# Ordering edges behind the low halves, and other paces for the depthwise convolution and its LayerNorm, in a two-layer decoder step

## The chip, the core and the metric

The kernel runs on one core of a Trainium2 chip. The metric is the device time of one execution in microseconds (us). Engines are named as in the profile: PE is TensorE's matmul stream and PEld its weight load, DVE is VectorE, ACT is ScalarE, POOL is GpSimd, SP is SyncE, which issues most transfers.

## What is computed

One inference step of a two-layer decoder trunk for 256 prompt tokens and 8 x 8 sample tokens, d_model 1024, all in float32. Each layer adds a half-weighted SwiGLU, a mixer with three branches (pooling, convolution, cross-attention into 256 memory tokens) and a second SwiGLU. The change touches the convolution branch. Cut to what matters:

```python
def conv_module(v, buf, w_dw, b_dw, ln_g, ln_b, w_pw):
    a, gate = jnp.split(v, 2, axis=-1)
    z = a * jax.nn.sigmoid(gate)
    ext = jnp.concatenate([buf.astype(z.dtype), z], axis=1)
    y = lax.conv_general_dilated(ext, w_dw[:, None, :], window_strides=(1,), padding='VALID',
        dimension_numbers=('NWC', 'WIO', 'NWC'), feature_group_count=CONV_WIDTH)   # 31 taps a channel
    y = jax.nn.silu(layernorm(y + b_dw, ln_g, ln_b))
    return y @ w_pw, ext[:, -CONV_BUF:]
...
def trunk_layer(x, ...):
    x = x + 0.5 * swiglu_ffn(rmsnorm(x, ffn1_norm), ffn1_w_gu, ffn1_w_down)
    h = rmsnorm(x, mix_norm)
    u, v, q, gl = jnp.split(h @ w_in, ...)
    merged = gates[:, :, 0] * y_pool + gates[:, :, 1] * y_conv + gates[:, :, 2] * y_att
    x = x + merged @ w_out
    x = x + 0.5 * swiglu_ffn(rmsnorm(x, ffn2_norm), ffn2_w_gu, ffn2_w_down)
```

## The kernel before

**Data and matmuls.** Channels lie on the 128 partitions in 8 blocks (`KB`), the T = 320 tokens (256 prompt, 64 sample) along the free axis. Every large matmul is done as three: a weight block is split into a high half `whi` and a low half `wlo`, the operand into `xh` and `xl`, and `chain` (L298) adds hi·xh + hi·xl for the blocks at hand (lines L306, L307) and then lo·xh (L309). A unit is 8 blocks of weights, so 24 matmuls of 128x320.

**Weights.** SyncE brings raw weights in pieces of 1 MB into 4 buffers (`Stream.issue`, L205), along with the sample group's keys (`in_kc`) and values (`in_vc`). A piece holds two units. `split` makes the halves three units ahead of use: the high half is a cast on ScalarE (L232), the low half a subtract on VectorE, raw minus high. VectorE's instructions all go through a helper, so all of them carry its line, L124. While `share` is on (in the parts that use `w_in`), every even unit takes another way: ScalarE casts the high half (L225) and writes its negative into the low half's place (L226), and GpSimd issues a transfer that accumulates onto it (L227).

**The mixer** goes through these parts in the order of the program: memory keys; the GLU part, which makes `z` block by block (`zfin`); memory values (`kv_values`); the queries; four pool groups, each with the columns `u` (copied to `ut`, L773), pool sums `us`, the gate of branch A, the prompt's softmax rows (`mx`, `sm`, `ex`, L602, L607) and the sample group's scores from the keys (L640); the gate of branch C in 8 steps (`sgc`, L831, L832), with the sample group's values (L665) and its output `exo` (L673), which TensorE transposes (L677); the gate of branch B in 8 steps (`sgb`, L861); the projection of the convolution branch, which reads `chi` and `clo`; and `w_out`.

**The convolution** runs beside all this. `conv_gen` (L541) is a generator. Two lanes (`conv_lane`, L494) each take every second of the 8 blocks: 31 taps a block, each one VectorE instruction that multiplies 256 columns of `z` by a constant and adds the running sum `cv` in PSUM; the second lane starts 15 steps late. GpSimd does the sample columns (`conv_sample`). Then come the sum over blocks `ysum`, the LayerNorm in some 13 steps (the mean and the variance by TensorE matmuls with ones, L354; subtraction, squares on ScalarE, reciprocal root on VectorE), and, after the third step of the gate of B, the scaling by `lnr`, Silu on ScalarE (L586) and the split into `chi` (L587) and `clo`.

**What sets the order.** The program is written in an order, and a scheduler then fixes each engine's list when the kernel is built. The written order comes from pacing: before each unit, `pump` gives every side task as many steps as its rate says, `RC` = 3.0 a unit for the convolution and its LayerNorm, `RN` = 6.0 from the Silu part on:

```python
task[2] += task[1]            # task = [generator, rate, credit]
while task[2] >= 1.0:
    task[2] -= 1.0
    if next(task[0], "end") == "end":
```

Of the kernel before, what the change touches and what calls it, by code (L numbers as in the profile page):

```python
# [7 lines left out]
F32 = mybir.dt.float32  # L8
# [3 lines left out]
ALU = mybir.AluOpType  # L12
# [5 lines left out]
TP = 256  # L18
# [14 lines left out]
LA = 3  # L33
NBIG = 8
C_LEAD = 24
RC = 3.0
RN = 6.0
RS = 2.0
RP = 2
# [1 line left out]
C_G1, C_GM, C_G2, C_GK, C_PS, C_BD, C_LG, C_LB, C_WD = 0, 8, 16, 24, 32, 40, 48, 56, 64  # L41
# [43 lines left out]
def trunk_kernel(  # L85
# [42 lines left out]
    dve = Timed(nc.vector, "dve", 1.04, 70.0)  # L128
    pool = Timed(nc.gpsimd, "pool", 2.2, 80.0)

    def nm(s):
        uid[0] += 1
        return f"{s}_{uid[0]}"
# [32 lines left out]
    def ccol(l, off, i):  # L166
        c = l * C_LAYER + off + i
        return cst[:, c:c + 1]
# [4 lines left out]
    class Stream:  # L173
# [45 lines left out]
        def split(self, u):  # L219
            c, half = seq[u // 2], u % 2  # L220
            raw = self.piece("w", c)[:, half * 1024:half * 1024 + 1024]
            hi = wp.tile([P, 1024], F32R, name=nm("whi"), tag="whi")
            lo = wp.tile([P, 1024], F32R, name=nm("wlo"), tag="wlo")
            if self.share and u % 2 == 0:
                nc.scalar.copy(hi[:, :], raw)  # L225
                nc.scalar.mul(lo[:, :], raw, -1.0)  # L226
                nc.gpsimd.dma_start(lo[:, :], w_in[c][:, half * 1024:half * 1024 + 1024], accum_op=ALU.add)  # L227
            else:
                n = 512 if u == 0 else 1024
                for e in range(0, 1024, n):  # L230
                    h, r = hi[:, e:e + n], raw[:, e:e + n]
                    nc.scalar.copy(h, r)  # L232
                    dve.tensor_tensor(out=lo[:, e:e + n], in0=r, in1=h.bitcast(F32), op=ALU.subtract)
            self.units[u] = (hi, lo)
            if half == 1:
                self.done("w", c)
# [37 lines left out]
    side = {}  # L274
# [20 lines left out]
            side.pop(name, None)  # L295

    ws = Stream()

    def chain(out, xs, n):

# [192 lines left out]
    def conv_lane(l, z, y, blocks, zdone, cdone):  # L493

        for j in blocks:
            while j not in zdone:
                yield
            zt = z[j // 4][:, j % 4, :]
            acc = psum("cv", 2)
            dve.tensor_scalar(out=acc[:, :TP], in0=zt[:, 0:TP], scalar1=ccol(l, C_WD, j), scalar2=ccol(l, C_BD, j),  # L500
                              op0=ALU.mult, op1=ALU.add)
            yield
            for k in range(1, TAPS):
                dst = acc[:, :TP] if k < TAPS - 1 else y[j][:, :TP]
                dve.scalar_tensor_tensor(out=dst, in0=zt[:, k:k + TP], scalar=ccol(l, C_WD, k * 8 + j),
                                               in1=acc[:, :TP], op0=ALU.mult, op1=ALU.add)
                yield
            cdone.append(j)

# [31 lines left out]
    def conv_gen(l, z, zdone, ch, gate):  # L541
# [6 lines left out]
        n = 0  # L548
# [11 lines left out]
        dve.tensor_tensor(out=ysum[:, :], in0=y[0], in1=y[1], op=ALU.add)  # L560
        for j in range(2, KB):
            dve.tensor_tensor(out=ysum[:, :], in0=ysum[:, :], in1=y[j], op=ALU.add)
        yield
        sc = tp.tile([P, 1280], F32, name=nm("lns"), tag="pr", bufs=1)
        work = [sc[:, i * T:(i + 1) * T] for i in range(4)]
# [9 lines left out]
        r = tp.tile([P, T], F32, name=nm("lnr"), tag="ysum", bufs=1)  # L575
# [6 lines left out]
        hi, lo = ch[0]  # L582
        for j in range(KB):
# [5 lines left out]
            if j > 0:  # L589
                dve.tensor_tensor(out=lo[:, j - 1, :], in0=y[j - 1], in1=hi[:, j - 1, :].bitcast(F32),  # L590
                                        op=ALU.subtract)
            yield
        dve.tensor_tensor(out=lo[:, KB - 1, :], in0=y[KB - 1], in1=hi[:, KB - 1, :].bitcast(F32),
                                op=ALU.subtract)
# [88 lines left out]
    def mixer(l, mh, acc, on_block):  # L683
# [27 lines left out]
        for j in range(KB):  # L711
# [7 lines left out]
            def zfin(j=j, pa=pa, sg=sg):  # L719
# [4 lines left out]
                if j == 0:  # L724
                    start("conv", conv_gen(l, z, zdone, ch, gate), RC)

# [162 lines left out]
    h, st, on_block = deferred_norm(0, C_G1, squares=False)  # L889
# [15 lines left out]
    for l in range(L):  # L905
# [16 lines left out]
        h, st, _ = mbox[0]  # L922
        mean = lambda st=st: mean_bc(st.acc[:, :], T)
        if l + 1 < L:
# [8 lines left out]
            h, st, _ = nxt[0]  # L933
# [128 lines left out]
```

## Time and profile before

| | |
|---|---|
| median of 3 runs | 1659.61 us (1659.60 to 1660.29) |
| the profiled execution | 1659.87 us, span 1657.9 us |
| granted TensorE clock, mean over the span | 0.997 |
| PE busy | 1630.5 us, 98% |
| DVE busy | 1120.4 us, 68% |
| ACT busy | 784.0 us, 47% |
| POOL busy | 266.7 us, 16% |

The span is the time from the first to the last instruction of the profiled execution; the device time is 2 us longer. A busy time is the sum over an engine's instructions, and a matmul's end is modelled, so TensorE's waits are read from the view of waits and not from its busy time. One layer's mixer takes its taps from 284 to 451 us, the other's from 1097 to 1266 us.

### The profile page before, as it was taken

How to read it: one execution, taken by the hardware profiler on the slowest of the kernel's cores; microseconds unless marked ns; L12 is line 12 of the kernel's file. 1: busy time of each engine (PE TensorE's matmuls, PEld its weight loads, DVE VectorE, ACT ScalarE, POOL GpSimd, SP SyncE). 2: the span in 40 equal slices, each digit the busy share in tenths (PEclk: the TensorE clock that was granted, in tenths of full speed). 3: DMA queues.
4: the chain of work that ended last, by engine and by line, in shares of the span. 5: the costliest groups of instructions: out<-in, count | busy, mean ns of one | idle time of the engine just before them, and what ended most of it. 6: DMA issues, size and time to landing. Idle time of an engine off the chain costs nothing.

```text
span 1657.9 us, 27271 instructions
## 1 busy us (share of the span) xinstructions
PE 1630.5 (98%) x11194; PEld 1585.8 (96%) x11194; DVE 1120.4 (68%) x1854; ACT 784.0 (47%) x1167; POOL 266.7 (16%) x292
## 2 busy tenths in 40 slices
PE   8999999999999999999999999999999999999996
PEld 7999999998889999999999999999988899999996
DVE  7555647999975675554565564579998757655543
ACT  5444534456665444443344443354566544444341
POOL 2000001677520000000000000046674000000000
PEclk9999999999999999999999999999999999999998
DMA  7444446978976444444444444577798754444430
GB/s 276 153 151 145 169 169 199 266 231 238 294 260 229 151 155 151 144 146 149 149 153 153 153 153 166 189 220 232 235 278 254 267 199 153 145 145 147 150 126 32
DMA packets 47325, 305.73 MB, mean 184 GB/s; under 512 B 5728, under 2 KB 5792, under 8 KB 14048
## 3 DMA queue, kind: packets, MB, share of 16 engines
q1 hardware_dynamic: 38160, 270.75, 45.4%
q0 software_dynamic: 8752, 32.90, 9.2%
q8 instruction: 88, 1.44, 0.3%
q10 hardware_dynamic: 288, 0.33, 0.1%
q14 instruction: 37, 0.30, 0.0%
HBM read 295.14 MB, written 8.82 MB: 183 GB/s over the span
## 4 chain that ended last, share of the span: by engine, by line
PE 86%; DVE 7%; issue 3%; DMA 3%; ACT 1%; POOL 0%; DVEq 0%; SPq 0%; ACTq 0%; POOLq 0%
PE mm L306 19%; PE mm L309 19%; PE mm L307 19%; PE cv L309 8%; PE cv L306 8%; PE cv L307 8%; DVE cv L124 3%; DMA raw<-in_kc 2%; DVE us L124 1%; DVE wlo L124 1%; PE sa L665 1%; PE mm L484 1%; PE mm L483 1%; PE mm L487 1%; PE st L837 1%
## 5 line engine op out<-in xcount | busy, mean ns | idle before, releaser
L124 DVE TENSOR_TENSOR wlo<-raw,whi 128x1024 fp32r<-128x1024 f32 (+1 forms) x403 | 498.6, 1238 | 196.2 <-PE mm L309 85.7
L232 ACT CAST whi<-raw 128x1024 fp32r<-128x1024 f32 (+1 forms) x403 | 420.6, 1045 | 428.3 <-PE mm L307 252.9
L306 PE MATMUL mm<-hhi,whi 128*128 128x320 f32 x1712 | 512.3, 313 | 7.6 <-ACT hhi L358 5.8
L307 PE MATMUL mm<-hlo,whi 128*128 128x320 f32 x1712 | 507.8, 310 | 0.0
L306 PEld LDWEIGHTS mm<-hhi,whi 128*128 128x128 f32 x1712 | 321.6, 188 | 16.2 <-ACT hhi L358 6.6
L307 PEld LDWEIGHTS mm<-hlo,whi 128*128 128x128 f32 x1712 | 321.8, 188 | 1.9 <-DVE hlo L124 0.6
L309 PE MATMUL mm<-hhi,wlo 128*128 128x320 f32 x1712 | 289.4, 310 | 1.7 <-DMA wlo<-in_w 1.7
L309 PEld LDWEIGHTS mm<-hhi,wlo 128*128 128x128 f32 x1712 | 260.4, 188 | 2.7 <-DMA wlo<-in_w 2.2
L124 DVE SCALAR_TENSOR_TENSOR cv<-z,cst,cv 128x256 f32<-128x256 f32 x464 | 194.6, 476 | 0.2
L307 PE MATMUL cv<-hlo,whi 128*128 128x320 f32 x592 | 175.0, 310 | 0.0
L306 PE MATMUL cv<-hhi,whi 128*128 128x320 f32 x592 | 173.9, 309 | 0.0
L124 POOL MEMSET z<- 128x120 f32 x4 | 0.8, 196 | 820.5 <-PE mm L307 820.5
L124 POOL TENSOR_TENSOR pr<-pr 128x512 f32<-128x512 f32 (+3 forms) x128 | 122.7, 959 | 7.2
L306 PE MATMUL mm<-hidh,whi 128*128 128x320 f32 x418 | 123.9, 309 | 0.0
L307 PE MATMUL mm<-hidl,whi 128*128 128x320 f32 x418 | 123.7, 309 | 0.0
L362 ACT CAST hidh<-up 128x320 fp32r<-128x320 f32 x88 | 40.0, 459 | 159.8 <-DVE up L124 159.8
L307 PEld LDWEIGHTS cv<-hlo,whi 128*128 128x128 f32 x592 | 111.0, 188 | 0.2
L306 PEld LDWEIGHTS cv<-hhi,whi 128*128 128x128 f32 x592 | 110.8, 188 | 0.0
L309 PE MATMUL cv<-hhi,wlo 128*128 128x320 f32 x592 | 98.8, 309 | 0.0
L309 PEld LDWEIGHTS cv<-hhi,wlo 128*128 128x128 f32 x592 | 89.9, 188 | 0.2
L124 DVE TENSOR_TENSOR up<-mm,rstd 128x320 f32<-128x320 f32 x53 | 26.0, 490 | 87.8 <-PE mm L309 87.8
L306 PE MATMUL cv<-hidh,whi 128*128 128x320 f32 x286 | 84.7, 309 | 0.0
(196 smaller groups left out, 2336.2 us busy)
## 6 DMA issues: line engine op xcount, KB each, us to landing
raw<-in_w SPq DMA_DIRECT2D x221, 1024.0 KB, 4.8
wlo<-in_w POOLq DMA_DIRECT2D x42, 512.0 KB, 7.1
raw<-in_kc SPq DMA_DIRECT2D x16, 1024.0 KB, 7.3
raw<-in_vc SPq DMA_DIRECT2D x16, 1024.0 KB, 6.0
out_co<-z POOLq DMA_DIRECT2D x16, 135.0 KB, 6.4
raw<-in_mem SPq DMA_DIRECT2D x2, 1024.0 KB, 4.8
out_mk<-kt POOLq DMA_DIRECT2D x2, 1024.0 KB, 5.1
out_mv<-va POOLq DMA_DIRECT2D x2, 1024.0 KB, 9.5
```

Of the source, the lines that this page charges most:

```text
L124: return op(*args, **kw)
L232: nc.scalar.copy(h, r)
L306: nc.tensor.matmul(out, hi, xh, start=(i + e == 0), stop=False)
L307: nc.tensor.matmul(out, hi, xl, start=False, stop=False)
L309: nc.tensor.matmul(out, lo, xh, start=False, stop=(i + e == last))
L362: nc.scalar.copy(hi, src)
L483: nc.tensor.matmul(pv[mb][:, :], mh[0][:, k, mb * P:mb * P + P], wh, start=(k == 0), stop=False)
L484: nc.tensor.matmul(pv[mb][:, :], mh[1][:, k, mb * P:mb * P + P], wh, start=False, stop=False)
L487: nc.tensor.matmul(pv[mb][:, :], mh[0][:, k, mb * P:mb * P + P], wl, start=False, stop=(k == KB - 1))
L665: nc.tensor.matmul(po[32 * h:32 * h + 32, :256], pp[:, at:at + 32], raw[:, mb * 1024 + h * 256:mb * 1024 + h * 256 + 256], start=(bb == 0 ...
L837: nc.tensor.matmul(pv[:, :TP], vt[:, mb, o * P:o * P + P], kt[:, 2 * hd + mb, :], start=(mb == 0), stop=(mb == 1))
```

## The change

The rate of the convolution's side task falls from 3.0 to 2.8 steps a unit. After the sum over blocks it is set to a new 4.0, so the LayerNorm's steps go faster, until `RN` = 6.0 applies as before. `split` keeps the last low half made on VectorE in `last_lo`, and a new function `behind` adds to each tap but the first of a block an ordering edge on that instruction. Both are on one engine, so the edge is no wait on the chip: it tells the scheduler that the tap must stand behind that low half in VectorE's list. Line numbers shift in the changed kernel (L124 becomes L125, L306 becomes L313, L673 becomes L682).

```diff
--- before.py
+++ after.py
@@ -33,7 +33,8 @@
 LA = 3
 NBIG = 8
 C_LEAD = 24
-RC = 3.0
+RC = 2.8
+RL = 4.0
 RN = 6.0
 RS = 2.0
 RP = 2
@@ -230,7 +231,7 @@
                 for e in range(0, 1024, n):
                     h, r = hi[:, e:e + n], raw[:, e:e + n]
                     nc.scalar.copy(h, r)
-                    dve.tensor_tensor(out=lo[:, e:e + n], in0=r, in1=h.bitcast(F32), op=ALU.subtract)
+                    self.last_lo = dve.tensor_tensor(out=lo[:, e:e + n], in0=r, in1=h.bitcast(F32), op=ALU.subtract)
             self.units[u] = (hi, lo)
             if half == 1:
                 self.done("w", c)
@@ -295,6 +296,12 @@
             side.pop(name, None)
 
     ws = Stream()
+
+    def behind(ins, earlier):
+
+        tc.add_manual_dep(ins.ins, earlier.ins.name,
+                          mybir.DependencyInfo(mybir.DependencyClass.NoSync, mybir.DependencyReason.DATA),
+                          reason="pace")
 
     def chain(out, xs, n):
 
@@ -502,8 +509,9 @@
             yield
             for k in range(1, TAPS):
                 dst = acc[:, :TP] if k < TAPS - 1 else y[j][:, :TP]
-                dve.scalar_tensor_tensor(out=dst, in0=zt[:, k:k + TP], scalar=ccol(l, C_WD, k * 8 + j),
+                tap = dve.scalar_tensor_tensor(out=dst, in0=zt[:, k:k + TP], scalar=ccol(l, C_WD, k * 8 + j),
                                                in1=acc[:, :TP], op0=ALU.mult, op1=ALU.add)
+                behind(tap, ws.last_lo)
                 yield
             cdone.append(j)
 
@@ -560,6 +568,7 @@
         dve.tensor_tensor(out=ysum[:, :], in0=y[0], in1=y[1], op=ALU.add)
         for j in range(2, KB):
             dve.tensor_tensor(out=ysum[:, :], in0=ysum[:, :], in1=y[j], op=ALU.add)
+        side["conv"][1] = RL
         yield
         sc = tp.tile([P, 1280], F32, name=nm("lns"), tag="pr", bufs=1)
         work = [sc[:, i * T:(i + 1) * T] for i in range(4)]
```

The order changes in these places. First, VectorE in the memory values of the first layer (`wlo` a low half, `cv<-z,cst,cv` a tap). Before:

```order
L124 TENSOR_TENSOR wlo_3381<-raw_3113,whi_3380 128x1024
L124 SCALAR_TENSOR_TENSOR cv_3194<-z_2729,cst,cv_3194 128x256
L124 TENSOR_TENSOR ysum_2807<-z_2729 128x320
L124 SCALAR_TENSOR_TENSOR cv_3387<-z_2729,cst,cv_3387 128x256
L124 TENSOR_TENSOR wlo_3408<-raw_3113,whi_3407 128x1024
L124 SCALAR_TENSOR_TENSOR cv_3194<-z_2729,cst,cv_3194 128x256
L124 TENSOR_TENSOR wlo_3437<-raw_3190,whi_3436 128x1024
L124 SCALAR_TENSOR_TENSOR cv_3387<-z_2729,cst,cv_3387 128x256
L124 SCALAR_TENSOR_TENSOR cv_3194<-z_2729,cst,cv_3194 128x256
L124 TENSOR_TENSOR wlo_3467<-raw_3190,whi_3466 128x1024
```

And with the change:

```order
L125 TENSOR_TENSOR wlo_3373<-raw_3109,whi_3372 128x1024
L125 SCALAR_TENSOR_TENSOR cv_3224<-z_2729,cst,cv_3224 128x256
L125 SCALAR_TENSOR_TENSOR cv_2997<-z_2729,cst,cv_2997 128x256
L125 TENSOR_TENSOR wlo_3395<-raw_3109,whi_3394 128x1024
L125 SCALAR_TENSOR_TENSOR cv_3224<-z_2729,cst,cv_3224 128x256
L125 SCALAR_TENSOR_TENSOR cv_2997<-z_2729,cst,cv_2997 128x256
L125 TENSOR_TENSOR wlo_3424<-raw_3184,whi_3423 128x1024
L125 SCALAR_TENSOR_TENSOR cv_3224<-z_2729,cst,cv_3224 128x256
L125 SCALAR_TENSOR_TENSOR cv_2997<-z_2729,cst,cv_2997 128x256
```

The taps between two low halves are two throughout, and the sum over blocks no longer has its first instruction there; over the GLU part the taps between two low halves fall from 9 to 13 down to 5 to 10, and 18 taps fewer have been issued when the memory values end. The taps end later in the program, in the gate of branch C.

Second, VectorE in the pool groups of the first layer, ahead of the low half that follows the second group's pool sums `us`. Before:

```order
L124 SCALAR_TENSOR_TENSOR merged_3908<-mm_4491,cst,merged_3908 128x320
L124 TENSOR_TENSOR us_4522<-us_4519 128x2x268
L124 TENSOR_TENSOR us_4522<-us_4519 128x2x160
L124 SCALAR_TENSOR_TENSOR cv_4230<-z_2730,cst,cv_4230 128x256
L124 SCALAR_TENSOR_TENSOR cv_3961<-z_2730,cst,cv_3961 128x256
L124 TENSOR_TENSOR us_4570<-us_4522 128x2x264
L124 TENSOR_TENSOR us_4570<-us_4522 128x2x128
L124 SCALAR_TENSOR_TENSOR cv_4230<-z_2730,cst,cv_4230 128x256
L124 TENSOR_TENSOR wlo_4552<-raw_4325,whi_4551 128x1024
```

And with the change:

```order
L125 SCALAR_TENSOR_TENSOR cv_4306<-z_2730,cst,cv_4306 128x256
L125 TENSOR_TENSOR us_4502<-us_4499 128x2x268
L125 TENSOR_TENSOR us_4502<-us_4499 128x2x160
L125 SCALAR_TENSOR_TENSOR cv_4046<-z_2730,cst,cv_4046 128x256
L125 SCALAR_TENSOR_TENSOR cv_4306<-z_2730,cst,cv_4306 128x256
L125 TENSOR_TENSOR us_4548<-us_4502 128x2x264
L125 TENSOR_TENSOR us_4548<-us_4502 128x2x128
L125 SCALAR_TENSOR_TENSOR cv_4046<-z_2730,cst,cv_4046 128x256
L125 TENSOR_TENSOR wlo_4532<-raw_4299,whi_4531 128x1024
```

It reads the same: of the 15 instructions between this low half and the one ahead of it, the change only swaps a `us` and a `merged`.

Third, ScalarE at the Silu block of the first layer (`z<-z,cst`), the gate of branch C (`sgc`, `va`) and the copy of the sample output, `exo`. Before:

```order
L586 ACTIVATE z_2730<-z_2730,cst 128x320 x3
L831 ACT_TABLE_LOAD
L831 ACTIVATE sgc_5204<-mm_5173 128x256
L832 ACTIVATE va_3351<-mm_5173 128x64
L831 ACTIVATE sgc_5263<-mm_5230 128x256
L832 ACTIVATE va_3351<-mm_5230 128x64
L232 CAST whi_5272<-raw_5228 128x1024
L232 CAST whi_5330<-raw_5228 128x1024
L831 ACTIVATE sgc_5300<-mm_5269 128x256
L832 ACTIVATE va_3351<-mm_5269 128x64
L673 COPY exo_5336<-sa_5172 128x256
```

And with the change:

```order
L595 ACT_TABLE_LOAD
L595 ACTIVATE z_2729<-z_2729,cst 128x320 x4
L233 CAST whi_5272<-raw_5222 128x1024
L595 ACTIVATE z_2730<-z_2730,cst 128x320 x2
L233 CAST whi_5330<-raw_5222 128x1024
L595 ACTIVATE z_2730<-z_2730,cst 128x320 x2
L840 ACT_TABLE_LOAD
L840 ACTIVATE sgc_5300<-mm_5269 128x256
L841 ACTIVATE va_3345<-mm_5269 128x64
L682 COPY exo_5336<-sa_5153 128x256
```

The block has moved behind two gates: it now starts after `sgc_5263` and ends right ahead of a table load, `sgc_5300` and the copy of `exo`. On TensorE, the transposes of that copy, before:

```order
L307 MATMUL mm_5327<-hlo_2484,whi_5176 128x320
L309 MATMUL mm_5327<-hhi_2483,wlo_5177 128x320 x8
L677 MATMUL st_5368<-cst,exo_5336 128x128 x2
L306 MATMUL mm_5363<-hhi_2483,whi_5233 128x320
L307 MATMUL mm_5363<-hlo_2484,whi_5233 128x320
```

And with the change:

```order
L314 MATMUL mm_5327<-hlo_2484,whi_5157 128x320
L316 MATMUL mm_5327<-hhi_2483,wlo_5158 128x320 x8
L313 MATMUL mm_5363<-hhi_2483,whi_5227 128x320
L314 MATMUL mm_5363<-hlo_2484,whi_5227 128x320
L686 MATMUL st_5368<-cst,exo_5336 128x128 x2
L313 MATMUL mm_5363<-hhi_2483,whi_5227 128x320
```

They have moved two matmuls back, into the next gate's chain. SyncE's list of transfers is the same in both.

## Rows read from the trace of the kernel before

**Rows 1.** The page's first part: busy us, share of the span, instructions.

```profile
PE 1630.5 (98%) x11194; PEld 1585.8 (96%) x11194; DVE 1120.4 (68%) x1854; ACT 784.0 (47%) x1167; POOL 266.7 (16%) x292
```

**Rows 2.** The page's groups by line: busy us, mean ns, idle before and its releaser.

```profile
L124 DVE TENSOR_TENSOR wlo<-raw,whi 128x1024 fp32r<-128x1024 f32 (+1 forms) x403 | 498.6, 1238 | 196.2 <-PE mm L309 85.7
...
L124 DVE SCALAR_TENSOR_TENSOR cv<-z,cst,cv 128x256 f32<-128x256 f32 x464 | 194.6, 476 | 0.2
```

**Rows 3.** Windows: length; PE, PEld, DVE, ACT, POOL busy (count); PEclk, DMA share, GB/s.

```profile
380.00:432.00 52.00, 50.62 (x371) 45.30 (x370) 50.98 (x110) 36.09 (x61) 36.62 (x43) 1.00 0.85 248
432.00:520.00 88.00, 86.99 (x660) 76.72 (x659) 70.51 (x134) 55.57 (x101) 19.09 (x21) 1.00 0.79 280
```

**Rows 4.** Waits of TensorE, 330 to 520 us: us in total, times, longest us.

```profile
PE mm L306 <- ACT ut L773: 0.7, 1, 0.7
PE mm L309 <- DMA wlo<-in_w: 0.7, 1, 0.7
PE st L652 <- ACT exs L607: 0.5, 1, 0.5
PE sa L640 <- DMA raw<-in_kc: 0.4, 1, 0.4
```

**Rows 5.** Waits of TensorE, 1145 to 1335 us.

```profile
PE sa L640 <- DMA raw<-in_kc: 2.5, 2, 1.7
PE mm L306 <- ACT ut L773: 1.4, 2, 1.0
```

**Rows 6.** Waits of TensorE's weight load, 330 to 520 us.

```profile
PEld mm L306 <- DVE wlo L124: 0.4, 1, 0.4
```

**Rows 7.** Timeline of ScalarE, then VectorE: start, us, engine, line, op, [idle before <- releaser].

```profile
432.63 1.05 ACT L232 CAST whi<-raw 128x1024 fp32r<-128x1024 f32 x1 [0.48 <-PE mm L307]
...
437.00 1.21 DVE L124 TENSOR_TENSOR wlo<-raw,whi 128x1024 fp32r<-128x1024 f32 x1
```

**Rows 8.** Timeline of ScalarE in the pool groups, first layer, then second.

```profile
383.13 1.28 ACT L602 ACT_TABLE_LOAD   x1 [6.00 <-DVE mx L124]
...
392.32 1.05 ACT L226 ACTIVATE wlo<-raw 128x1024 fp32r<-128x1024 f32 x1
...
1240.25 0.51 ACT L607 ACTIVATE exs<-exs,sm 128x256 f32<-128x256 f32 x1 [0.83 <-DVE sm L124]
```

**Rows 9.** The chain of waits, 436 to 460 and 1250 to 1270 us: start, us, what.

```profile
436.12 1.17 PE mm L309 x8
...
439.55 11.62 DMA raw<-in_kc
...
1253.67 14.16 DMA raw<-in_kc
```

**Rows 10.** Timeline of the DMA issues on SyncE, then on GpSimd.

```profile
430.39 8.17 SPq L205 DMA_DIRECT2D raw<-in_w  x2
438.65 1.28 SPq L205 DMA_DIRECT2D raw<-in_kc  x2
...
440.93 0.87 POOL L227 DMA_DIRECT2D wlo<-in_w  x1 [0.39 <-issue]
```

**Rows 11.** Window in which the key pieces land, columns as in rows 3.

```profile
448.00:452.00 4.00, 3.61 (x32) 2.25 (x30) 3.93 (x6) 2.42 (x5) 3.90 (x4) 1.00 1.04 351
```

**Rows 12.** Timeline of ScalarE at the Silu block, then of TensorE at the transposes.

```profile
498.42 1.74 ACT L586 ACTIVATE z<-z,cst 128x320 f32<-128x320 f32 x3
500.18 1.28 ACT L831 ACT_TABLE_LOAD   x1
501.47 0.38 ACT L831 ACTIVATE sgc<-mm 128x256 f32<-128x256 f32 x1
...
508.89 0.37 ACT L673 COPY exo<-sa 128x256 f32<-128x256 f32 x1 [1.91 <-PE sa L665]
...
512.37 0.38 PE L677 MATMUL st<-cst,exo 128*128 128x128 f32 x2
```

**Rows 13.** The tile `chi`: weight loads that read it, ns, first and last start.

```profile
L306 PEld LDWEIGHTS mm<-chi,whi x128: 187/188/188, 537.1 to 1380.1; 128*128 128x128 f32 x128
```

## The prediction

> **What bounds the kernel now.** I read the page first, then the stretch in which the taps run, then the waits inside it. The page [rows 1] shows TensorE busy for 98% of the span and VectorE for 68%, so in the mean VectorE has room. The groups by line [rows 2] show what stands side by side on VectorE: 403 low halves of 1.24 us each, and 464 conv taps, 194.6 us together, so 0.42 us a tap. The windows [rows 3] show where the room is missing: from 380 to 432 us VectorE is busy for 98% of the time (50.98 of 52.00 us). There the taps, the softmax rows, the pool sums and the low halves stand in one full queue. In the stretch behind it there is room again (70.51 of 88.00).
>
> The question is whether TensorE pays for that full queue. Its waits [rows 4, 5] answer it: in the stretch with taps and LayerNorm it waits four times in the first layer, 2.3 us together, and four times in the second, 3.9 us. None is for a low half that VectorE made: three are for `ut`, one for `exs`, one for a low half that comes by an accumulating transfer, three for the sample group's keys `raw<-in_kc`. On the weight load's side one wait of 0.4 us for VectorE's low half is listed [rows 6], and no matmul is listed as held by it. So **the change has 6.2 us to win at the most, 0.37% of the time, and 2.9 us of that (0.4 + 2.5) are for the keys' transfers.** The other 3.3 us are 0.2%, which is also about what a measurement of this kernel can tell from no change.
>
> **The sum, part by part.** No arithmetic goes or comes: the same taps, low halves and matmuls are there in another order, and an edge within one engine is no instruction. Both cost 0. What moves is when things happen.
>
> *The low halves.* Fewer taps stand ahead of each in the GLU part, so they come earlier there. By the end of the value part 18 taps have been put off, 18 x 0.42 = 7.6 us of VectorE. Since no matmul waited for these low halves, earlier ones are worth 0. The nearest to a late one stands at 437.00 us: its high half is ready at 432.63 + 1.05 = 433.68, so the subtract starts 3.3 us late [rows 7]. Between it and the low half ahead the new order has the same 15 instructions (the second pair of lists in the change), so it can gain some tenths at most.
>
> *`ut` and the accumulating transfer.* These waits hang on VectorE at second hand. ScalarE stands still for 6.00 us ahead of 383.13 for `mx`, which is queued on VectorE among the taps; the write that must precede the accumulating transfer follows in ScalarE's queue at 392.32 [rows 8]. In the second layer the scaling of `exs` waits 0.83 us for `sm` at 1240.25, and `ut` stands behind it. With up to 7.6 us less ahead of them, `mx` and `sm` come earlier. But from there on VectorE works through the same list and is as full as before until the taps end, so only the part put off is won. For the transfer's wait (0.7) I take −0.4, between 0 and −0.7. Of the 2.1 us for `ut` (0.7 + 1.4) I take about a third, −0.75, between 0 and −2.1, because ScalarE's own work in its queue holds `ut` too. For `exs` (0.5) I take 0: its transposes move behind the next low halves, while the sum over blocks leaves the stretch; between −0.5 and +0.6.
>
> *The sample keys.* The chain of waits [rows 9] leads from both key waits back to TensorE itself. One transfer takes 11.62 us from 439.55, when TensorE has read the key buffer that it refills, the other 14.16 us from 1253.67. No tap stands in that chain. In the first layer SyncE issues two key pieces at 438.65, behind two weight pieces, and the accumulating transfer goes out at 440.93 [rows 10]. If that one goes earlier or later, the keys' transfer shortens or stretches. I take −0.3. The bounds: −2.9 where both waits end, and +2.0 where the first layer's transfer becomes as long as the second's (14.16 − 11.62 = 2.5, less some tenths that stay hidden).
>
> By a rule of the Trainium skill ("Perfetto Trace Analysis", section "Roofline") one core's 16 DMA engines give about 435 GB/s together; by that an estimate for the 3.67 MB in flight there (two weight pieces, two key pieces, half a piece accumulated) is 8.4 us, and the keys would come in time, −2.9 instead of −0.3. In the trace the window in which they land shows 351 GB/s at a DMA share of 1.04 [rows 11]: there it stays below the figure with the engines full.
>
> *The LayerNorm.* From the first tap to the sum over blocks the generator takes 139 steps (15 until the second lane starts, then 4 x 31). At 3.0 a unit that is 46.4 units, at 2.8 it is 49.7, 3.3 more. A unit is 24 matmuls; 8 take 1.17 us [rows 9], so a unit takes 3.5 us and the delay is 11.6 us. Some 13 steps of the LayerNorm at 4 rather than 3 a unit give back 1.1 units, 3.8 us. Net it is 7.8 us later. In the trace the Silu block ends at 498.42 + 1.74 = 500.16 [rows 12]; it now ends near 508, or at 511 if the higher pace gives little. In the new order it stands right ahead of a table load, a gate and the copy of `exo` (1.28 + 0.38 + 0.37 = 2.0 us), so the copy is done between 510 and 513. TensorE's transposes of `exo` ran at 512.37 and move two matmuls back, to 512.7. That makes a new wait of 0 to 0.3 us a layer; I take 0.3 for both together, between 0 and 0.6. The projection that reads the LayerNorm's result starts at 537.1 [rows 13], more than 20 us behind, so its lateness costs nothing there.
>
> Sum: −0.4 − 0.75 + 0 − 0.3 + 0.3 = −1.15 us. The profiled execution took 1659.87 us, 0.26 us above the median of three (1659.61). From its own time the sum gives 1658.7, and against the median 1658.5 us, which I forecast.
>
> **Rivals.**
> 1. *The keys come in time too.* With all the waits of rows 4 and 5 gone it is −6.2 + 0.3 = −5.9, so 1653.7 us; with the other terms as in my sum and only the keys' waits gone, −1.15 + 0.3 − 2.9 = −3.75, 1655.9 us. For it: moving one transfer can take it out of the burst. Against it: SyncE's list is the same, and TensorE itself releases these loads. Chance 0.14.
> 2. *ScalarE is freed wholly.* All waits but the keys' end and `exo` costs nothing: −3.3, 1656.3 us. For it: each of them has a `mx`, a `sm` or the write for a transfer behind it. Against it: VectorE is as full afterwards. Chance 0.12.
> 3. *The Silu block becomes the wait (slower).* If it ends later than 512.7 − 2.0 = 510.7 us, TensorE's in-order queue stands at the `exo` transposes, with the next gate's matmuls behind them. Were the LayerNorm 4 us later than I worked out, because the edges also hold taps behind low halves that are late themselves, the block would end at 512 to 515: 1.3 to 4.3 us a layer. With my other terms (−1.45) that is +1.1 to +7.1, so 1660.8 to 1666.8 us, 1663.8 in the middle. For it: in the new order the copy stands behind the whole block. Against it: a tap lags only as far as its low half does. Chance 0.22.
> 4. *Nothing that counts.* TensorE waits for nothing that is moved: 1659.6 us. I count this with the forecast, 0.52 together.
>
> **How the numbers follow.** Faster by over 0.2% (below 1656.3) is rival 1 and half of rival 2: 0.20. Slower by over 0.2% (above 1662.9) is two thirds of rival 3: 0.15. All the rest, 0.65, is the same. The forecast's own bounds are 1656.3 (all its gains but the keys': −0.7 − 2.1 − 0.5) and 1662.8 (all its losses at once: +0.6 + 2.0 + 0.6). The range for 8 in 10 goes on from there, to 1655.0, which takes in a half of rival 1, and to 1663.5, which takes in almost a half of rival 3: 0.07 and 0.12 are left out.
>
> **What would show it.** Right: VectorE still about 98% busy from 380 to 432 us; no matmul that waits for a low half; shorter waits for `ut` and for the accumulating transfer; a wait for `exo` of at most some tenths near 513 us; the keys' waits where they were. Wrong: the keys' waits gone, or their transfer near 14 us in both layers; a wait for `exo` of over 1.3 us; or a new wait of TensorE for `sm`, `plh` or `pll`, which would mean that VectorE was relieved in one place and became the bound in the next.

## The result, and the profile after

The changed kernel takes 1674.66 us (median of 4 runs, 1671.60 to 1675.45) against 1659.61 us before: ratio 1.0087, 95% interval 1.0075 to 1.0100, so 0.9% slower. The profiled execution took 1675.45 us, 15.6 us more than the one of before.

The busy times of the page, to be read against [rows 1]:

```profile
PE 1635.5 (98%) x11194; PEld 1590.2 (95%) x11194; DVE 1134.1 (68%) x1854; ACT 784.9 (47%) x1167; POOL 272.9 (16%) x292
```

VectorE runs the same 1854 instructions and needs 1134.1 us for them instead of 1120.4. That is the first thing to see: no work was added, and 13.7 us were. The windows that answer to [rows 3], and three of 4 us in the second of them:

```profile
380.00:432.00 52.00, 50.90 (x374) 45.80 (x374) 52.00 (x107) 33.14 (x55) 34.34 (x36) 1.00 0.82 254
432.00:520.00 88.00, 82.48 (x610) 71.49 (x605) 75.50 (x143) 50.56 (x88) 29.03 (x32) 0.96 0.74 252
476.00:480.00 4.00, 3.44 (x11) 3.09 (x12) 3.89 (x8) 2.28 (x7) 0.00 (x0) 0.50 0.66 272
480.00:484.00 4.00, 4.00 (x42) 2.90 (x40) 3.42 (x7) 1.39 (x2) 0.00 (x0) 0.70 0.01 4
484.00:488.00 4.00, 4.00 (x33) 3.79 (x26) 0.22 (x1) 0.00 (x0) 0.00 (x0) 1.00 0.85 309
```

VectorE has not become freer from 380 to 432 us (52.00 of 52.00), GpSimd is busier from 432 to 520 us (29.03 us against 19.09), and TensorE's granted clock is at 0.50, its lower level of 1.2 GHz, from 476 to 480 us. TensorE's waits, in the stretches of [rows 4, 5], the first layer first:

```profile
PE st L661 <- ACT exs L616: 3.0, 1, 3.0
PE mm L313 <- ACT ut L782: 2.3, 2, 1.2
PE sa L649 <- DMA raw<-in_kc: 1.2, 1, 1.2
PE mm L316 <- DMA wlo<-in_w: 1.1, 1, 1.1
```

```profile
PE st L661 <- ACT exs L616: 4.9, 1, 4.9
PE mm L313 <- ACT ut L782: 2.1, 2, 1.7
PE sa L649 <- DMA raw<-in_kc: 0.6, 1, 0.6
```

The wait for `exs`, 0.5 us before and listed in the first layer alone, is now 3.0 and 4.9 us. Lined up matmul by matmul against the trace of before, between points at which both kernels have done the same matmuls, the changed kernel goes from 4.4 us late (the last matmul ahead of the first `exs` transposes, at 467.0 us before) to 9.2 us late (480.7 us), and from 8.5 (1280.0 us) to 16.3 us (1295.7 us) around the second: it loses 4.8 and 7.8 us there, together 12.6 of 15.6 us.

How the stop comes about is read on four engines. VectorE first (start, us, engine, line, operation; what stands between is left out):

```profile
459.72 2.75 DVE L125 TENSOR_TENSOR us<-us 128x536 f32<-128x536 f32 x2
...
464.26 2.77 DVE L125 TENSOR_TENSOR wlo<-raw,whi 128x1024 fp32r<-128x1024 f32 x1
466.95 1.99 DVE L125 TENSOR_TENSOR us<-us 128x512 f32<-128x512 f32 x2
...
471.04 0.42 DVE L125 TENSOR_REDUCE mx<-sa 128x1 f32<-128x256 f32 x1
...
472.50 0.14 DVE L125 TENSOR_SCALAR mx<-mx 128x1 f32<-128x1 f32 x1
...
474.71 0.15 DVE L125 RECIPROCAL sm<-sm 128x1 f32<-128x1 f32 x1
```

GpSimd beside it:

```profile
459.51 4.15 POOL L125 TENSOR_TENSOR pr<-pr 128x512 f32<-128x512 f32 x4
...
464.12 1.83 POOL L125 TENSOR_TENSOR pr<-z,cst 128x960 f32<-128x960 f32 x1
...
466.52 1.67 POOL L125 TENSOR_TENSOR pr<-pr 128x512 f32<-128x512 f32 x1
```

ScalarE, and the TensorE instructions that wait for it:

```profile
470.74 0.73 ACT L813 CAST plh<-us 128x640 fp32r<-128x640 f32 x1 [5.67 <-DVE us L125]
471.37 1.05 ACT L233 CAST whi<-raw 128x1024 fp32r<-128x1024 f32 x1
472.44 1.28 ACT L611 ACT_TABLE_LOAD   x1
473.73 0.47 ACT L611 ACTIVATE exs<-sa,mx 128x256 f32<-128x256 f32 x1
474.10 0.19 ACT L611 ACTIVATION_READ_ACCUMULATOR exs<-sa,mx 128x1 f32 x1
474.31 1.28 ACT L840 ACT_TABLE_LOAD   x1
475.61 0.38 ACT L840 ACTIVATE sgc<-mm 128x256 f32<-128x256 f32 x1
475.89 0.22 ACT L841 ACTIVATE va<-mm 128x64 f32<-128x64 f32 x1
475.99 0.51 ACT L616 ACTIVATE exs<-exs,sm 128x256 f32<-128x256 f32 x1
```

```profile
476.56 0.69 PE L661 MATMUL st<-cst,exs 128*128 128x128 f32 x2 [3.02 <-ACT exs L616]
...
479.28 0.47 PE L314 MATMUL mm<-pll,whi 128*128 128x320 f32 x1
479.55 0.47 PE L313 MATMUL mm<-plh,whi 128*128 128x320 f32 x1
```

VectorE is still making taps between the pool sums `us` of the last group, and its low half at 464.26 takes 2.77 us instead of 1.21 [rows 7] while a product on GpSimd runs from 464.12 for 1.83 us. ScalarE stands idle for 5.67 us for `us`, then goes through `plh`, a cast, a table load, the exponential, a second table load and a gate before it can scale `exs` at 475.99. TensorE reaches the transposes of `exs` 3.02 us too early. Behind the stop its matmuls start 0.27 us apart (479.28 and 479.55) where 8 took 1.17 us before [rows 9].

A part of the lateness is ScalarE's own list. In the kernel before, the scaling stood ahead of the second table load:

```profile
467.32 0.51 ACT L607 ACTIVATE exs<-exs,sm 128x256 f32<-128x256 f32 x1
...
468.08 1.28 ACT L831 ACT_TABLE_LOAD   x1
```

Now `sm` is done at 474.71 + 0.15 = 474.86 and the scaling starts 1.1 us after it, behind that load and the gate.

### The profile page after: what moved, and what is told of

Its sections match the earlier page's. It is cut to its first block, busy times and chain, and to the rows that moved or that the text cites. A ratio compares the mean times of both kernels' runs of the same rounds, so it can differ in the third digit from the quotient of the medians.

```text
span 1673.7 us, 27270 instructions
## 1 busy us (share of the span) xinstructions
PE 1635.5 (98%) x11194; PEld 1590.2 (95%) x11194; DVE 1134.1 (68%) x1854; ACT 784.9 (47%) x1167; POOL 272.9 (16%) x292
## 4 chain that ended last, share of the span: by engine, by line
PE 79%; DVE 15%; issue 3%; DMA 1%; ACT 1%; POOL 0%; DVEq 0%; SPq 0%; POOLq 0%; ACTq 0%
PE mm L316 17%; PE mm L313 17%; PE mm L314 17%; PE cv L316 8%; PE cv L313 8%; PE cv L314 8%; DVE cv L125 7%; DVE wlo L125 3%; DVE us L125 3%; PE sa L674 1%; PE mm L494 1%; PE mm L490 1%; PE mm L491 1%; PE st L846 1%; DVE ysum L125 1%
## 5 line engine op out<-in xcount | busy, mean ns | idle before, releaser
L125 DVE TENSOR_TENSOR wlo<-raw,whi 128x1024 fp32r<-128x1024 f32 (+1 forms) x403 | 505.3, 1255 | 194.6 <-PE mm L316 84.0
L313 PE MATMUL mm<-hhi,whi 128*128 128x320 f32 x1712 | 512.0, 313 | 8.3 <-ACT hhi L365 6.8
L313 PEld LDWEIGHTS mm<-hhi,whi 128*128 128x128 f32 x1712 | 321.6, 188 | 16.5 <-ACT hhi L365 7.0
L125 DVE SCALAR_TENSOR_TENSOR cv<-z,cst,cv 128x256 f32<-128x256 f32 x464 | 198.3, 477 | 0.8
L313 PE MATMUL cv<-hhi,whi 128*128 128x320 f32 x592 | 173.9, 309 | 0.0
L125 POOL MEMSET z<- 128x120 f32 x4 | 0.8, 196 | 821.8 <-PE mm L314 821.8
L125 POOL TENSOR_TENSOR pr<-pr 128x512 f32<-128x512 f32 (+3 forms) x128 | 127.7, 998 | 7.7
L313 PE MATMUL mm<-hidh,whi 128*128 128x320 f32 x418 | 123.9, 309 | 0.0
L313 PEld LDWEIGHTS cv<-hhi,whi 128*128 128x128 f32 x592 | 110.7, 188 | 0.0
L125 DVE TENSOR_TENSOR up<-mm,rstd 128x320 f32<-128x320 f32 x53 | 26.0, 490 | 87.8 <-PE mm L316 87.8
L313 PE MATMUL cv<-hidh,whi 128*128 128x320 f32 x286 | 84.7, 309 | 0.0
```

The lines of the kernel that those rows point to most:

```text
L125: return op(*args, **kw)
L313: nc.tensor.matmul(out, hi, xh, start=(i + e == 0), stop=False)
```

## The experiments

The theory: the edges pin the taps to their place in the program, those put off land among the last pool sums, there they and GpSimd's late sample sums delay `exs`, TensorE stops, and its clock falls. The rivals: the pace alone does it; the higher pace of the LayerNorm does it; a full VectorE would take the time at another wait anyway; GpSimd's work, not the taps, is what delays `exs`. All runs compute everything unless their expectation says what is left out; the filled stop adds matmuls. The kernel before took 1659.9 to 1660.4 us beside them.

| run | median us | ratio to before, 95% interval |
|---|---|---|
| the pace of 2.8 alone | 1664.68 | 1.0027 (1.0018 to 1.0037) |
| the edges alone | 1665.41 | 1.0031 (1.0019 to 1.0044) |
| edges and pace, no RL | 1678.57 | 1.0106 (1.0091 to 1.0122) |
| the change again | 1674.55 | 1.0086 (1.0071 to 1.0101) |
| edges, RL, pace of 4.0 | 1668.70 | 1.0052 (1.0037 to 1.0067) |
| the change, late transposes | 1666.29 | 1.0037 (1.0022 to 1.0052) |
| before, late transposes | 1660.97 | 1.0003 (0.9993 to 1.0012) |
| the change, filled stop | 1678.74 | 1.0113 (1.0097 to 1.0128) |
| the change, no sums on GpSimd | 1651.22 | 0.9948 (0.9933 to 0.9963) |
| before, no sums on GpSimd | 1654.08 | 0.9963 (0.9950 to 0.9975) |
| before, GpSimd freed | 1668.50 | 1.0048 (1.0033 to 1.0063) |
| the change, GpSimd freed | 1676.40 | 1.0095 (1.0080 to 1.0110) |
| the same, held, 1.0 steps | 1671.99 | 1.0073 (1.0056 to 1.0089) |
| the same, held, 1.25 steps | 1682.70 | 1.0135 (1.0119 to 1.0150) |
| before, freed and held, 1.0 steps | 1662.08 | 1.0010 (1.0000 to 1.0019) |
| before, freed and held, 1.25 steps | 1675.80 | 1.0093 (1.0078 to 1.0108) |

### The parts of the change

The pace alone. Edit, from the changed kernel:

```diff
-                behind(tap, ws.last_lo)
...
-        side["conv"][1] = RL
```

> Only the lower pace of 2.8 steps a unit; no edges, LayerNorm at the same 2.8. In VectorE's list as many taps stand ahead of the sample softmax as before (240 of 240 in the last pool group). Theory (the edges bind the taps to their place, and taps among the last pool sums delay exs): 1659.6 us within 1.5, TensorE's wait for exs at 0.5 us. Rival (the pace alone puts the taps off): about 1674 us, with the wait of 3 and 5 us for exs.

Measured: 1664.68 us. The `exs` wait stays at 0.5 us in the first layer, as the theory has it, and is 1.3 us in the second. But the time is 5 us above the theory's, for another reason, a wait for `exo`:

```profile
PE st L684 <- ACT exo L680: 2.0, 1, 2.0
...
PE st L659 <- ACT exs L614: 0.5, 1, 0.5
```

Without the higher pace the LayerNorm comes late, ScalarE's Silu block stands ahead of the copy of `exo`, and TensorE waits for it (2.0 us here, 1.2 us in the second layer). Behind this stop, too, the granted clock is lower for a while:

```profile
516.00:520.00 4.00, 3.73 (x16) 3.74 (x17) 1.75 (x2) 3.97 (x7) 0.00 (x0) 0.57 0.27 115
```

This is rival 3 of the prediction, in a kernel that has only a part of the change.

The edges alone. Edit, from the changed kernel:

```diff
-RC = 2.8
+RC = 3.0
...
-        side["conv"][1] = RL
```

> Only the edges; 3.0 steps a unit as before, no higher pace for the LayerNorm. In VectorE's list 237 of 240 taps stand ahead of the last sample softmax, where the changed kernel has 231 and the kernel before 240. [...] Rival (the pace is what costs): 1659.6 us.

Measured: 1665.41 us, a part of the loss and inside the 1661 to 1668 us that were expected, but by another wait. `exs` costs 1.0 us a layer and `ut` 3.4 us a layer:

```profile
405.09 1.28 ACT L610 ACT_TABLE_LOAD   x1 [7.95 <-DVE mx L125]
...
408.23 0.43 ACT L781 COPY ut<-mm 128x320 f32<-128x320 f32 x1
```

```profile
408.72 0.63 PE L313 MATMUL mm<-plh,whi 128*128 128x320 f32 x1 [3.37 <-ACT ut L781]
```

Before, `ut` stood behind this softmax as well, but the table load was done by the time `mx` came:

```profile
399.96 1.28 ACT L602 ACT_TABLE_LOAD   x1
402.63 0.47 ACT L602 ACTIVATE ex<-st,mx 128x256 f32<-128x256 f32 x1 [1.39 <-DVE mx L124]
...
403.54 0.43 ACT L773 COPY ut<-mm 128x320 f32<-128x320 f32 x1
```

With the edges the load itself starts only behind `mx` (7.95 us idle ahead of it), and a cast stands between the exponentials and `ut`; VectorE also makes `mx` 2.4 us later (done at 405.01 against 402.59 us). `ut` starts 4.7 us later, and TensorE waits for it. Here too the granted clock falls (0.93 in the window from 380 to 432 us).

Edges and pace without the LayerNorm's higher pace. Edit, from the changed kernel:

```diff
-        side["conv"][1] = RL
```

> Edges and the pace of 2.8, but the LayerNorm at 2.8 too. Up to the sum over blocks the order is that of the changed kernel. Theory: 1674 us within 2.5, the same waits for exs (3.0 and 4.9 us) and the same fall of the clock. Rival (the LayerNorm's higher pace crowds VectorE and ScalarE and costs the time): 1660 to 1666 us. If the later Silu block made TensorE wait for exo, it would be seen here first: over 1 us a layer at the exo transposes.

Measured: 1678.57 us, 4 us above the change itself. The `exs` waits are 2.9 and 5.1 us, and the `exo` waits are back with 2.3 and 1.4 us. So the higher pace of the LayerNorm is the part that helps: it takes the `exo` wait away that the lower pace makes. (Alone, in the kernel before, it was not run.) The clock differs from the change's:

```profile
432.00:520.00 88.00, 82.50 (x629) 71.82 (x622) 76.63 (x146) 50.01 (x86) 29.38 (x32) 1.00 0.77 263
```

Behind the first stop of 2.9 us it stayed at 1.00 here, where it fell behind the change's 3.02 us.

What the pace and the edges do to VectorE's list shows in the number of taps ahead of the sample softmax of the second and of the last pool group, out of 240:

```
before; pace alone               202   240
edges at 3.0                     194   237
edges at 2.8 (the change)        187   231
edges at 4.0                     200   240
```

Without edges the pace moves no tap here; with them it does. The change again, and edges with a pace at which all taps stand ahead of the last softmax once more (RC = 4.0 in the changed kernel):

> The changed kernel itself once more, beside the three kernels of this group on one chip: 1674.7 us within 2, the waits for exs at 3.0 and 4.9 us.

> The edges and the LayerNorm at 4.0, with the convolution at 4.0 steps a unit too. In VectorE's list all 240 taps stand ahead of the last sample softmax again, as in the kernel before. Theory (what costs is where the edges pin the taps, not the edges as such): no wait for exs over 1 us and no fall of the clock there, 1658 to 1663 us. Rival (any list built with the edges makes ScalarE's queue stand behind mx, as in the run with the edges alone): a wait for ut of 2 to 4 us a layer, 1664 to 1668 us.

Measured: 1674.55 us with `exs` waits of 3.3 and 5.1 us, and 1668.70 us. At 4.0 no wait for `exs` is listed, but one for `ut` of 3.8 us in the first layer and 2.4 us in the second, and 3.3 us for accumulating transfers in the second. With the last taps back in their place the wait for `exs` is gone, as the theory has it; but GpSimd's work from 432 to 520 us is back too (19.41 us), so this run alone does not tell which of the two matters. The time is the rival's, a little above its range: this list with edges is slower too, by `ut`.

### The stop and the clock

The transposes put behind a later matmul by an edge. Edit, the same in the changed kernel and in the kernel before (`late` is set for the last group):

```diff
+            if late:
+                behind(tt, ws.last_mm)
...
-            if o == 0:
+            if o == 2:
                 drain("ss")
```

> The changed kernel, but the transposes of the last exs are held by an edge behind the third step of the gate of C, about 8 us later in TensorE's list; the taps stay where they are. Theory (all of the loss is TensorE's stop at those transposes and the clock that falls behind it): the waits of 3.0 and 4.9 us and the stretch at 1.2 GHz go, 13 to 14 us less, about 1661 us within 1.5. Rival (VectorE is the bound there, so a wait for plh, sgc or merged takes its place): 1668 to 1674 us. Second rival (the clock falls on its own, without the stop): about 1667 us, with the granted clock still at 0.5 near 476 us.

> The kernel before, with the transposes of the last exs held by an edge behind the third step of the gate of C. Theory: the wait of 0.5 us for exs goes and nothing else, 1659.2 us within 0.8, the same within the measurement. Rival (the later transposes push the sample output and its exo wait): 1661 to 1664 us.

Measured: 1666.29 us, 8.4 us less than the change, where 13 to 14 were expected, and 1660.97 us, the same as before. The `exs` waits are gone and the clock stays at 1.00 from 432 to 520 us. A part of the time comes back at the next thing that ScalarE does late, the gate's `va`, which frees TensorE's PSUM buffer:

```profile
PE mm L313 <- ACT ut L784: 2.6, 2, 1.4
...
PE mm L313 <- ACT va L843: 1.1, 1, 1.1
```

The wait for `va` is 1.1 us here and 2.3 us in the second layer. So taking the stop at `exs` and its clock away gives back rather more than half of the loss; the rest stays as the same lateness of VectorE and ScalarE, at `va`, `ut` and the accumulating transfers.

Filling the stop with matmuls that nobody reads, to see whether the clock then stays up:

```diff
+        if fill is not None:
+            du = pst()
+            for e in range(24):
+                fm = nc.tensor.matmul(du[:, :T], fill[:, :P], fill, start=True, stop=True)
+                behind(fm, ws.last_mm)
```

> The changed kernel, with 24 matmuls of 128x320 that nobody reads put on TensorE right ahead of the last exs transposes, which stand one matmul and one gate product later for it. Work added: 2 x 24 x 0.147 = 7.0 us. [...]

Measured: 1678.74 us, where 1665 to 1669 us were expected if the stop were filled: a failed experiment. The added matmuls need a PSUM buffer that VectorE frees late (`sgc`), so TensorE stood still 1.9 us ahead of them in the first layer and 4.0 us in the second. In the first layer, with stops of 1.9 and 0.7 us and work between them, the clock stayed at 1.00 (window 432 to 520 us), and in the second, with 4.0 us, it fell (0.96 from 1250 to 1335 us). Since it also stayed at 1.00 behind 2.9 us in the run without the higher pace, this does not show that the filling kept it up.

### GpSimd's sums

The sums of the sample columns left out on GpSimd:

```diff
-                    pool.tensor_tensor(out=pr[:, 0:m, :], in0=pr[:, 0:m, :], in1=pr[:, m:2 * m, :], op=ALU.add)
```

> The changed kernel without the additions of the sample columns' convolution on GpSimd (their sums are left out; the multiplications and the copies stay). The taps in VectorE's list are as in the changed kernel (231 of 240 ahead of the last sample softmax). Theory A (the taps put off are what delays exs): the waits for exs stay at 2 us and more, 1668 to 1674 us. Theory B (GpSimd's work, which lies beside the last pool sums, stretches VectorE's low half to 2.77 us and its sums, some 5 us together): these are back at 1.2 us, the waits for exs are gone, 1659 to 1663 us.

> The kernel before without GpSimd's additions of the sample columns' convolution (left out as in the run of the changed kernel without them, which took 1651.2 us). Theory A (the change costs only through GpSimd's work beside VectorE's list, the place of the taps alone costs nothing): 1651 us within 1.5 here too. Theory B (where GpSimd is quiet the edges do what they are for, and the low halves and softmax rows come earlier): 1653 us or more here. Theory C (the taps' place costs by itself as well): 1649 us or less.

Measured: 1651.22 us for the change without the sums, 1654.08 us for the kernel before without them. The taps stand where they stood (231 of 240), GpSimd is busy for 10.58 us from 432 to 520 us, and the low half and the sums behind it are short again:

```profile
457.45 1.21 DVE L125 TENSOR_TENSOR wlo<-raw,whi 128x1024 fp32r<-128x1024 f32 x1
458.59 0.89 DVE L125 TENSOR_TENSOR us<-us 128x512 f32<-128x512 f32 x2
```

```profile
PE mm L316 <- DMA wlo<-in_w: 0.6, 1, 0.6
```

No wait for `exs`, `ut` or the keys is left, though ScalarE's list still has the second table load ahead of the scaling. Theory A falls; theory B has the waits right, and its 1659 to 1663 us 8 us too high. **With the sums left out the change costs nothing; it takes the change and GpSimd's sums together to lose the time.** If anything the change then gains, 1651.22 against 1654.08 us on different chips, but the intervals of the two ratios overlap, and the kernel before without the sums has waits for `exo` of 0.9 and 1.0 us, which the higher pace takes away. The sums are left out everywhere, so the run does not tell those beside the last pool sums from the earlier ones. VectorE's taps, with one input from PSUM, take 0.48 us either way; what stretches are its instructions with two inputs from SBUF. The Trainium skill ("SBUF — State Buffer", section "Who interferes with whom") states it so: a VectorE instruction with two SBUF inputs contends with a GpSimd instruction that reads SBUF, and the one that comes second is blocked. The trace agrees: the low half of 464.26 us, which starts 0.14 us behind GpSimd's product, takes 1.56 us longer, about what was left of that product (1.69 us); in the second layer one that starts at 1286.19 us, 0.14 us into such a product, takes 2.78 us.

So, in kernels that compute everything, can GpSimd be moved? GpSimd waits for a block's taps before it takes the next block. The edit writes its last sum into columns of `z` that nobody reads any more and copies them later:

```diff
+                    dst = z[j // 4][:, j % 4:j % 4 + 1, ZW - TS:ZW] if m == 1 and half == 1 else pr[:, 0:m, :]
-            while j not in cdone:
-                yield
-            nc.scalar.activation(y[j][:, TP:T], pr[:, 0, :], AF.Identity, bias=ccol(l, C_BD, j))
+            summed.append(j)
```

> The kernel before, with the sums of the sample columns written by GpSimd's last addition into columns of z that nobody reads any more, so that GpSimd does not wait for a block's taps before it takes the next block; all arithmetic as before. GpSimd's work should end near the end of the GLU and value parts instead of near 450 us. Theory (GpSimd's work beside VectorE's two-input instructions is what the last pool groups suffer from): the waits for ut, exs and the keys in the pool groups fall, 1654 to 1659 us. Rival (the same work only moves into the GLU part, and the accumulating transfers that GpSimd issues come later): 1660 to 1666 us, with longer waits for wlo<-in_w.

> The changed kernel with the same freeing of GpSimd from the taps. Theory: GpSimd is quiet when the last pool sums run, VectorE's low half there takes 1.2 us instead of 2.77, the waits for exs fall from 3.0 and 4.9 to under 1 us and the clock stays up: 1656 to 1663 us. Rival (the taps put off are enough for the loss): 1670 us or more.

Measured: 1668.50 and 1676.40 us, both worse than without it, with the longer waits for the accumulating transfers that the first's rival names. In the changed kernel the `exs` waits are gone, with the taps where they were:

```profile
432.00:520.00 88.00, 88.00 (x673) 77.59 (x672) 72.18 (x158) 58.32 (x104) 8.53 (x12) 1.00 0.81 274
```

```profile
PE mm L316 <- DMA wlo<-in_w: 7.5, 3, 6.8
PE mm L313 <- ACT ut L786: 2.4, 1, 2.4
```

But GpSimd also issues the accumulating transfers, in order with its sums, and while it is full TensorE waits 6.8 us for one of them in the first layer and 5.4 us in the second; in the kernel before so changed, 6.0 and 4.2 us (there ScalarE's write was done at 363.31 us, and the transfer was issued at 368.17 us, behind three instructions of the sums). So TensorE comes late: the matmuls ahead of the first `exs` transposes are 11.8 us behind the kernel before, where the change's are 4.4, and `exs` is ready later than in the change, at 479.5 against 476.5 us. That its wait is gone says nothing here about GpSimd beside the pool sums.

The last four runs hold the sums behind those transfers by the same kind of edge, at a lower pace of the sample part (RS = 1.0 or 1.25):

```diff
-                nc.gpsimd.dma_start(lo[:, :], w_in[c][:, half * 1024:half * 1024 + 1024], accum_op=ALU.add)
+                self.last_acc = nc.gpsimd.dma_start(lo[:, :], w_in[c][:, half * 1024:half * 1024 + 1024], accum_op=ALU.add)
...
+                    behind(pool.tensor_tensor(out=dst, in0=pr[:, 0:m, :], in1=pr[:, m:2 * m, :], op=ALU.add), ws.last_acc)
```

> The changed kernel with GpSimd freed from the taps, its sample products and sums held behind the last accumulating transfer by ordering edges, at 1.0 step a unit. Theory (the loss needs GpSimd's work beside VectorE's last pool sums; the taps' place alone costs little): no wait for exs over 1 us, waits for the accumulating transfers of 2 us a layer at most, 1657 to 1664 us. Rival (the taps put off are enough): exs waits of 2 us and more, 1668 us or more. If the spread-out GpSimd work still reaches into the last pool sums, the exs wait stays in part and the time lies between.

> As the run before, at 1.25 steps a unit: GpSimd's sums end earlier, ahead of the last pool sums, and lie more densely beside the accumulating transfers. Theory: no exs wait; waits for the accumulating transfers of 1 to 4 us a layer; 1658 to 1666 us. Rival: 1668 us or more with exs waits.

> The kernel before with the same GpSimd at 1.0 step a unit. Theory (late accumulating transfers were what made the freed GpSimd slower at 1668.5 us): the waits of 6.0 and 4.2 us for them go to 1 us or less and the waits of the pool groups stay small: 1655 to 1660 us. Rival (GpSimd's sums beside VectorE cost the same wherever they lie): 1660 to 1668 us.

> As the run before, at 1.25 steps a unit. Theory: between the two, a wait for the accumulating transfers of up to 3 us a layer, 1656 to 1663 us; the pool groups' waits smaller than at 1.0, since GpSimd is done earlier.

Measured: 1671.99, 1682.70, 1662.08 and 1675.80 us, none within its theory's range. At 1.25 the longest wait for an accumulating transfer is still 6.1 us in the changed kernel and 4.2 us in the kernel before. At 1.0 it falls to 1.2 and 0.3 us in the first layer, but the sums reach into the last pool group again, and with them the `exs` wait:

```profile
432.00:520.00 88.00, 84.95 (x643) 74.10 (x642) 75.30 (x148) 53.75 (x96) 26.10 (x26) 0.98 0.77 258
```

```profile
PE mm L313 <- ACT ut L786: 3.7, 2, 2.7
PE st L665 <- ACT exs L620: 2.0, 1, 2.0
```

Set side by side, the five lists with the taps at 231 of 240 and the transposes in their place order themselves by what GpSimd does from 432 to 520 us: 29.03 us busy with an `exs` wait of 3.0 us, 26.10 with 2.0, and 11.26 (the pace of 1.25), 10.58 (no sums) and 8.53 (freed) with none listed. Two of the five carry no weight: at 1.25 as in the freed kernel TensorE is late by then (12.8 us behind, and `exs` ready at 480.5 us). At 1.0 the 2.0 us and the time are what its rival (the taps are enough) has, but GpSimd is not quiet there, so it decides nothing. The evidence that GpSimd's work is needed for this wait is the run without the sums, in which TensorE is early (1.0 us ahead of the kernel before) and `exs` is ready at 467.0 us; that no kernel that computes everything shows it stays open. No list that computes everything beat the kernel before.

## Why the prediction was wrong, point by point

The forecast was 1658.5 us, the range 1655.0 to 1663.5; it took 1674.66 us.

- **What bounds the kernel.** Right as far as it went: VectorE stayed full from 380 to 432 us, and no matmul waits for a low half that VectorE made. Wrong was what followed from it. The cap of 6.2 us bounds what a change can win from the waits there are; it says nothing of the waits that it can make.
- **The step that failed: `exs`, "I take 0 ... between −0.5 and +0.6".** It measured 3.0 + 4.9 − 0.5 = +7.4 us. I had counted 18 taps put off as 7.6 us won ahead of `mx` and `sm`, and had not followed them to where they go: by the lists, 9 of 240 stand behind the last sample softmax, and more between the pool sums ahead of it, in a stretch where VectorE's queue decides when ScalarE gets to `exs`; and ScalarE's new list has a table load and a gate ahead of the scaling. "The sum over blocks leaves the stretch" was the wrong reason, too: one of its instructions, 1.51 us long, lies in it.
- **No term for GpSimd.** Its sums wait for the taps of their block, so they moved along with them, from 19.09 to 29.03 us in the stretch, and stretched VectorE's two-input instructions. The runs without the sums show that the loss needs GpSimd's sums.
- **No term for the clock.** A wait was priced at its length. Around the first stop 4.8 us were lost, 2.5 of them the longer wait; behind it TensorE takes 5.8 us (476.56 to 482.34) for matmuls that took 3.1 us before, and that is the rest. Over both layers 7.4 of the 12.6 us are waits, which leaves about 5.2 for the work at 1.2 GHz.
- **`ut` and the accumulating transfer**, −0.75 and −0.4: of the wrong sign. `ut` rose from 2.1 to 4.4 us, the transfers within the first layer's stretch from 0.7 to 1.1. ScalarE's list was built anew, and with it the softmax's table load can come behind `mx` (7.95 us idle ahead of it in the run with the edges alone).
- **The sample keys**, −0.3: measured 1.8 us in all against 2.9, so −1.1, within the bounds. The 3.67 MB of the estimate beside it is one weight piece, two key pieces and half a piece; the other weight piece had landed at 436.04 us.
- **The LayerNorm and `exo`**, +0.3: right in mechanism. The Silu block ended at 519.17 us, and 9.2 us of that are TensorE's own delay by then, so at 510 on the time of before, between the 508 and 511 that were worked out; no wait for `exo` is listed. The runs without the higher pace show the wait that rival 3 described, at 1.2 to 2.3 us a layer.
- **The rivals.** Slower was given 0.15, by way of `exo`. It came by way of `exs`, through the same in-order queues. The list of what would prove the forecast wrong named a wait for `sm`, `plh` or `pll`; the wait came one step later, at what is made from `sm`.

Not settled: why the clock fell behind some stops and not behind others of the same length (below); how much of the late `exs` is taps, how much GpSimd and how much ScalarE's new list; and why the lists with edges at 3.0 and 4.0 have the table load behind `mx`.

## What to carry to other kernels

When a change puts work off, follow it to where it lands and price it there: on every engine that waits for that one, in order, with the neighbour that shares its memory path, and not only by what is freed where it left. An upper bound on the gain from the waits that a profile lists is no bound on the loss, and a new stop of TensorE can cost, beside its length, a slow stretch behind it (about 2.6 us here). A pace in the program may move nothing until an ordering edge makes the scheduler keep it, so the two have to be tried apart.

## What the hardware showed that was not expected

A stop of TensorE of 3.02 us was followed by matmuls at 1.2 GHz (granted clock 0.50 from 476 to 480 us, 0.70 in the next 4 us, 1.00 after that). The length of a stop did not tell it by itself: in the runs here one of 2.02 us was followed by the lower clock (the pace alone), and one of 1.73 us too (before with late transposes, 1269.99 us), while one of 2.89 us (no RL, 476.91 us) and one of 1.74 us (the kernel before, 1267.88 us) were not. The same 1854 VectorE instructions took 13.7 us longer in another order, as more of those with two SBUF inputs ran beside GpSimd: 1.21 us became 2.77 us for one low half, the 403 together took 505.3 us instead of 498.6, and the 24 pool sums `us<-us` 27.1 instead of 23.0. Such stretching is not new: the kernel before has a low half of 2.68 us at 333.23 us, at a place where nothing waited for it. With GpSimd's sums left out, 120 us of its busy time (272.9 against 152.9 us), the changed kernel was 8.8 us faster than the kernel before with all its work (1651.22 against 1659.99 us), and the kernel before without them 6.3 us faster than with them (1654.08 against 1660.41 us).
